# Eight experts with places of their own size, taken in the order of their rows

## The chip, the cores and the metric

The kernel runs on one NeuronCore of a Trainium2 chip. The metric is the device time of one execution in microseconds. Five engines share the work: TensorE (PE, with its weight loads shown as PEld), VectorE (DVE), ScalarE (ACT), GpSimd (POOL) and SyncE (SP), which issues transfers. Each takes its instructions in the order in which they were written into its queue and waits for others by semaphores.

## The reference

Two layers of a post-normalised encoder on 512 tokens of 1024 features, in float32. Each layer mixes tokens (three mixers in parallel, merged by gates) and then channels: the first layer by a dense SwiGLU, the second by eight experts, of which each token takes two. The change is in the experts alone:

```python
def moe_swiglu(h2, w_router, w_gate, w_up, w_down):
    logits = (h2 @ w_router).astype(jnp.float32)
    top_logits, top_idx = lax.top_k(logits, TOP_K)        # TOP_K = 2 of N_EXPERTS = 8
    top_w = jax.nn.softmax(top_logits, axis=-1)
    ...
    hid = jax.nn.silu(lax.ragged_dot(xs, w_gate, sizes)) * lax.ragged_dot(xs, w_up, sizes)
    y = lax.ragged_dot(hid, w_down, sizes)                # D_EXP = 3584
    y = y * top_w.reshape(-1)[order][:, None].astype(y.dtype)
    return jnp.zeros_like(h2).at[tok].add(y.astype(h2.dtype))
```

512 tokens with two experts each make 1024 rows, 128 per expert on average. With the inputs used, the experts 0 to 7 get 136, 132, 144, 108, 129, 114, 124 and 137 rows.

## The kernel before

Mixers, dense FFN and the second mixers take the first 2090 us. The expert stage (function `moe`) takes the rest.

Float32 products are made of two parts. Every weight chunk comes raw by a transfer on SP (`Stream.load`, L191, two chunks of 128x1024 or 128x896 in one, five buffers). ACT rounds it to the product's fp32 format (whi, L204), DVE takes what is left in half precision (wlo, L205). Four chunks of parts exist: the two in use and two ahead. PE multiplies whi with both parts of the rows (2 x 144 columns, `gu<-xg,whi`) and wlo with the rows in half precision (144 columns, `gu<-xh,wlo`), all at L276.

*Routing* (L1139 to L1190): the two best experts of each token as one-hot masks `oh`, their sum `sel`, the place of a token among the rows of its expert `rank`. `gather_rows(e)` makes the row indices of an expert (o1, ii, ix) and reads its rows from DRAM by address (xt, POOL, L1189); `gather_turn` turns them to columns (xg, xh; L1205 to L1208) in two blocks, of 128 and 16 rows.

*Places*: every expert has CAP = 144 rows. If one has more, the loop of L1240 runs `overflow` for 128 further rows of it, as often as the count `nxi` says; with these inputs no round runs.

*An expert* (`expert`, from L1308) has 28 steps f of gate and up: two chunks (gate and up), 32 products into `gu`. After them ACT copies the low part (gt, L1317), DVE adds the high part (gt, L1318), ACT makes the silu (gs, L1320), POOL multiplies by up (gs, L1321), ACT rounds (hd, L1323), DVE takes the rest (hd, L1324) and POOL makes the half-precision copy (hh, L1327). Then 16 pairs of chunks of down: 14 + 14 products a pair into `mx`, with yt (ACT L1345, DVE L1346) after every second pair. `turn_out` turns yt to rows (ys, L1299) and ACT's queue writes them to `ybuf` (L1303), or `ylast` for the last expert (L1301). The next expert's rows are gathered from step 8 on, turned from step 18 on.

*The end*: during the last expert the rows of the other seven are fetched from ybuf (POOL, L1358, eight gathers yg with three buffers) and added with their weights (DVE, acc, L1360). The last expert's own rows follow in two halves (`combine_last`, L1377 to L1383), with the statistics of the norm (L343), and then the last LayerNorm goes to the output.

*What sets the order*: PE's order is the order of the program. The queues of ACT, DVE, POOL and SP are ordered by the compiler's scheduler, which has its own estimates of every instruction's duration. So a change of shapes can change the order in which the engines take their work.

Of the kernel before, what the change touches and what calls it, by code (L numbers as in the profile page):

```python
# [21 lines left out]
P = 128  # L22
# [17 lines left out]
CAP = 144  # L40
# [101 lines left out]
def constants():  # L142
# [23 lines left out]
    c["eidx"] = np.ascontiguousarray(np.broadcast_to(np.stack([NE - e, e * CAP], 0)[None], (P, 2, NE))).astype(np.float32)  # L166
# [7 lines left out]
class Stream:  # L174
    """weight chunks in order of use, each split into a rounded part and the exact rest"""
# [57 lines left out]
def body(tc, A, out, dbg=None):  # L233
# [27 lines left out]
    class PE:  # L261
        """matmuls in the order of emission, with a rough count of the time they take"""
# [25 lines left out]
    def soon(after, fn, *a):  # L288
        """matmul work on results of other engines: run between chunks once they had time to come"""
# [12 lines left out]
            # the task whose results were begun last holds the most buffers  # L302
# [75 lines left out]
    def need(*js):  # L378
        """the token tiles that the next products read"""
# [4 lines left out]
    def settle():  # L384
        """after the first product on a norm's output: its buffers are free"""
# [13 lines left out]
    # feature-major product of one 128-column chunk  # L399
# [10 lines left out]
    # the first chunks after a norm, half of the tokens at a time  # L410
# [18 lines left out]
    # token-major product, n columns, per k-tiles a chunk; the last four chunks a token tile at a time  # L429
# [64 lines left out]
    # ---------------------------------------------------------------- weights  # L494
# [7 lines left out]
    # ------------------------------------------------------------ first norm  # L502
# [53 lines left out]
    def route_consts():  # L556
# [17 lines left out]
        eidx = load_const("eidx", [P, 2, NE], pool=rp_)  # L574
# [82 lines left out]
    def hgrn_head(pool, h, cmask, fkq, v, g):  # L657
        # running products inside blocks that double: c up to t, e after s
# [319 lines left out]
    def overflow(pool, more, pairs, hsrc, acc):  # L978
        """the next P rows of an expert that has more than CAP: which one follows from the count of rounds"""
        step, rounds = more  # L980
# [18 lines left out]
        V.tensor_scalar(at[:, 1:2], at[:, 1:2], float(P), float(CAP), op0=OP.mult, op1=OP.add)  # L999
# [3 lines left out]
        V.tensor_scalar(here, eidx[:, 0], at[:, 0:1], None, op0=OP.is_equal)  # L1003
        ow = pool.tile([P, 3, NJ], F32, name="ow")
# [43 lines left out]
        def load(ap):  # L1048
            raw = pool.tile([P, 2048], F32, name="oraw", bufs=3)
# [45 lines left out]
        y = pool.tile([P, D], F32, name="oy")  # L1095
# [25 lines left out]
    def moe(hT, g_ap, b_ap):  # L1121
# [13 lines left out]
        with tc.tile_pool(name="route", bufs=1, side="right") as mp, ExitStack() as psg_:  # L1135
            hsrc = hbuf[0]
            blocks = [(0, P), (P, CAP - P)]
# [36 lines left out]
            def gather_rows(e):  # L1174
                xts = []
                o1 = mp.tile([P, NJ, CAP], BF, name="o1", bufs=2)
                for j in range(NJ):
                    V.tensor_scalar(o1[:, j], iota, rank[:, j, e:e + 1], sel[:, j, e:e + 1],
                                    op0=OP.is_equal, op1=OP.mult)
                for b0, bn in blocks:  # L1180
# [18 lines left out]
            def gather_turn(xs, xts, b, kk):  # L1199
                (b0, bn), xt, (xg, xh) = blocks[b], xts[b], xs  # L1200
# [10 lines left out]
            turns_in = [(b, kk) for b in range(len(blocks)) for kk in range(2)]  # L1211
            xts = gather_rows(0)
            stream.fill()
            # softmax over the two
# [8 lines left out]
            # rounds of P more rows that the experts need beyond CAP  # L1223
            pc = psM.tile([P, NE], F32, name="mx")
            for j in range(NJ):
                T.matmul(pc, ones, selb[:, j], start=(j == 0), stop=(j == NJ - 1))
            rounds = mp.tile([P, NE], F32, name="rounds")
            V.tensor_scalar(rounds, pc, float(CAP), None, op0=OP.is_gt)
            for r in range(1, (S - CAP + P - 1) // P):
                V.tensor_scalar(ms2, pc, float(CAP + P * r), None, op0=OP.is_gt)  # L1230
                V.tensor_tensor(rounds, rounds, ms2, OP.add)
            nxi = mp.tile([P, 1], I32, name="nxi")
# [6 lines left out]
            n_more = nc.values_load(nxi[0:1, 0:1], min_val=0, max_val=NE * ((S - CAP + P - 1) // P),  # L1239
                                    skip_runtime_bounds_check_because="a sum of comparisons")  # L1240
            with tc.tile_pool(name="over", bufs=1) as op_:
                with tc.For_i(0, n_more, 1):
                    overflow(op_, (step, rounds), (oh, wt, rank, sel), hsrc, acc)

            xg = new_x()
            for b, kk in turns_in:
                gather_turn(xg, xts, b, kk)
            dump("xg", xg[0][:, :, 0].bitcast(F32))
            # rows of the expert outputs, one per choice; the last expert's come separately
# [3 lines left out]
            V.tensor_scalar(ms[:, 4], rank[:, :, NE - 1], float(CAP - 1), None, op0=OP.min)  # L1253
            V.tensor_copy(sl7, ms[:, 4])
            for i in range(2):
                V.tensor_tensor(t1, rank, oh[:, i], OP.mult)
                V.tensor_reduce(ms[:, 4], t1, AX.X, OP.add)
                V.tensor_scalar(ms[:, 5], ms[:, 4], float(CAP), None, op0=OP.is_lt)
# [22 lines left out]
            def flat(ps):  # L1281
                return ps[:, :2 * CAP].rearrange("p (a c) -> p a c", a=2)
# [11 lines left out]
            def turn_out(e, kk, yt, ys):  # L1294
                for (b0, bn), y in zip(blocks, ys):
# [6 lines left out]
                    elif kk:  # L1302
                        SC.dma_start(ybuf[e * CAP + b0:e * CAP + b0 + bn], y[:bn])  # L1303
# [4 lines left out]
            def expert(e, xs, at):  # L1308
                xg, xh = xs
                hid = []  # L1310
                for f in range(KE):
                    ps = psG.tile([P, 2, 512], F32, name="gu", bufs=2)
                    ws = stream.take(2)
                    accumulate([(flat(ps[:, q]), ws[q], lambda k: (xg[:, k], xh[:, k]), True, True)
                                for q in range(2)], KD)
                    t = bp.tile([P, 2, CAP], F32, name="gt", bufs=2)
                    SC.activation(t, ps[:, :, CAP:2 * CAP], AF.Copy)  # L1317
                    V.tensor_tensor(t, ps[:, :, :CAP], t, OP.add)  # L1318
                    s = bp.tile([P, CAP], F32, name="gs", bufs=2)
                    SC.activation(s, t[:, 0], AF.Silu, scale=1.0 / (WS * XS))  # L1320
                    G.tensor_tensor(s, s, t[:, 1], OP.mult)  # L1321
                    hd = bp.tile([P, 2, CAP], FR, name="hd", bufs=KE + 6)
# [3 lines left out]
                    hh = bp.tile([P, CAP], F16, name="hh", bufs=KE + 6)  # L1326
# [5 lines left out]
                for _ in blocks:  # L1332
# [3 lines left out]
                for d in range(KD):  # L1336
                    ps = psM.tile([P, 512], F32, name="mx")
                    pv = flat(ps)
# [119 lines left out]
```

## Time and profile before

| | us |
|---|---|
| three runs | 3321.95, 3325.41 (median), 3325.93 |
| span of the profiled execution | 3321.9 |
| first expert's gate/up begins at | 2124.0 |
| gate/up of an expert, 0 to 7 | 101.3, 96.6, 96.6, 97.5, 96.6, 95.5, 95.5, 105.7 |
| down of an expert | 46.5, the last 53.8 |
| from the last down product to the end | 33.6 |

The profiled execution's span is its own time. The rows that stand in a section below come from this one execution. A view called "timeline" gives start, duration, engine, line, operation, and in brackets the idle time of the engine just before and what ended it. "Windows" gives, for stretches of the span, the busy time of each engine with its number of instructions, the granted clock of TensorE as a share of full speed (1.00 is 2.4 GHz, 0.50 is 1.2 GHz), the busy share of the 16 DMA engines and their GB/s.

### The profile page before, as it was taken

How to read it: one execution, taken by the hardware profiler on the slowest of the kernel's cores; microseconds unless marked ns; L12 is line 12 of the kernel's file. 1: busy time of each engine (PE TensorE's matmuls, PEld its weight loads, DVE VectorE, ACT ScalarE, POOL GpSimd, SP SyncE). 2: the span in 40 equal slices, each digit the busy share in tenths (PEclk: the TensorE clock that was granted, in tenths of full speed). 3: DMA queues.
4: the chain of work that ended last, by engine and by line, in shares of the span. 5: the costliest groups of instructions: out<-in, count | busy, mean ns of one | idle time of the engine just before them, and what ended most of it. 6: DMA issues, size and time to landing. Idle time of an engine off the chain costs nothing. (4 is left out here: it accounts for less than half of the span.)

```text
span 3321.9 us, 53257 instructions
## 1 busy us (share of the span) xinstructions
PE 3167.9 (95%) x20782; PEld 2760.0 (83%) x20782; DVE 2091.5 (63%) x2862; ACT 1737.9 (52%) x2993; POOL 851.4 (26%) x901
## 2 busy tenths in 40 slices
PE   7999899999999999999999999799999999999985
PEld 6778788888888888677788888699999999999985
DVE  5766633344533245667433344698898989889896
ACT  4754323422322225744323322487787878878774
POOL 1233401111100010335201111253342524325253
PEclk9999999999999999999999999799999999999997
DMA  5112232233323332122222223689898898988984
GB/s 175 45 55 88 64 103 70 95 95 126 118 95 99 129 108 95 46 67 70 83 89 83 89 92 117 219 312 329 309 322 320 302 330 311 331 316 313 337 295 179
DMA packets 109588, 566.63 MB, mean 171 GB/s; under 512 B 12624, under 2 KB 12672, under 8 KB 80656
## 3 DMA queue, kind: packets, MB, share of 16 engines
q1 hardware_dynamic: 97344, 522.23, 45.3%
q10 hardware_dynamic: 7344, 25.69, 2.1%
q0 software_dynamic: 4640, 15.22, 1.3%
q8 instruction: 165, 2.70, 0.3%
q14 instruction: 95, 0.78, 0.1%
HBM read 547.89 MB, written 15.20 MB: 170 GB/s over the span
## 5 line engine op out<-in xcount | busy, mean ns | idle before, releaser
L205 DVE SCALAR_TENSOR_TENSOR wlo<-raw,whi 128x1024 f16<-128x1024 f32 (+1 forms) x704 | 858.6, 1246 | 75.6 <-ACT whi L204 75.2
L208 ACT ACTIVATE whi<-raw 128x1024 fp32r<-128x1024 f32 x314 | 332.6, 1060 | 833.5 <-PE acc L276 710.4
L204 ACT ACTIVATE whi<-raw 128x1024 fp32r<-128x1024 f32 (+1 forms) x704 | 707.7, 1012 | 97.3 <-PE mx L276 86.9
L209 DVE TENSOR_TENSOR wlo<-raw,whi 128x1024 fp32r<-128x1024 f32 x314 | 435.5, 1388 | 509.7 <-ACT whi L208 481.2
L276 PE MATMUL gu<-xg,whi 128*128 128x288 f32 x3584 | 536.3, 302 | 24.6 <-DVE gt L1318 23.2
L276 PEld LDWEIGHTS gu<-xg,whi 128*128 128x128 f32 x3584 | 486.6, 189 | 37.2 <-DVE gt L1318 24.2
L276 PE MATMUL acc<-hThi,whi 128*128 128x512 f32 (+1 forms) x1312 | 509.9, 389 | 2.3 <-ACT hThi L326 2.3
L276 PE MATMUL acc<-hTlo,whi 128*128 128x512 f32 (+1 forms) x1312 | 506.4, 386 | 1.6 <-DVE hTlo L327 1.6
L276 PE MATMUL acc<-hThi,wlo 128*128 128x512 f32 (+1 forms) x1312 | 506.2, 386 | 0.0
L1321 POOL TENSOR_TENSOR gs<-gs,gt 128x144 f32<-128x144 f32 x224 | 224.4, 1002 | 576.9 <-ACT gs L1320 546.7
L276 PEld LDWEIGHTS <-wlo 128*128 128x128 f16 x5376 | 333.6, 98 | 39.3 <-DVE wlo L205 13.7
L276 PEld LDWEIGHTS acc<-hThi,whi 128*128 128x128 f32 x1312 | 248.7, 190 | 55.1 <-issue 4.9
L276 PEld LDWEIGHTS acc<-hTlo,whi 128*128 128x128 f32 x1312 | 248.6, 190 | 49.4 <-DVE hTlo L327 1.8
L276 PEld LDWEIGHTS acc<-hThi,wlo 128*128 128x128 f32 x1312 | 248.5, 189 | 49.4
L276 PE MATMUL mx<-hd,whi 128*128 128x288 f32 x1792 | 270.2, 300 | 6.4 <-DVE hd L1324 6.4
L276 PE MATMUL gu<-xh,wlo 128*128 128x144 f16 x3584 | 264.8, 227 | 6.0 <-DVE wlo L205 6.0
L276 PEld LDWEIGHTS mx<-hd,whi 128*128 128x128 f32 x1792 | 241.7, 188 | 8.4 <-DVE hd L1324 8.2
L276 PE MATMUL acc<-whi,hThi 128*128 128x512 f32 (+1 forms) x576 | 224.7, 390 | 0.1
L276 PE MATMUL acc<-whi,hTlo 128*128 128x512 f32 (+1 forms) x576 | 220.5, 383 | 3.3 <-DVE hTlo L327 3.3
L276 PE MATMUL acc<-wlo,hThi 128*128 128x512 f32 (+1 forms) x576 | 220.0, 382 | 2.8 <-DVE wlo L209 2.8
L1327 POOL CAST hh<-hd 128x144 f16<-128x144 f32 x224 | 171.2, 764 | 90.4 <-ACT hd L1323 90.4
L357 POOL TENSOR_TENSOR ln_r<-ln_r,ln_b 128x512 f32<-128x512 f32 x26 | 42.0, 1631 | 446.7 <-DVE ln_r L356 441.5
(263 smaller groups left out, 4554.2 us busy)
## 6 DMA issues: line engine op xcount, KB each, us to landing
raw<-in_w_gu SPq DMA_DIRECT2D x224, 1024.0 KB, 5.3
raw<-in_w_l SPq DMA_DIRECT2D x248, 512.0 KB, 3.5
raw<-in_w_dn SPq DMA_DIRECT2D x128, 896.0 KB, 4.7
raw<-in_w_ffn SPq DMA_DIRECT2D x66, 512.0 KB, 3.5
hspillm<-ln_r ACTq DMA_DIRECT2D x8, 512.0 KB, 2.6
ybuf<-ys ACTq DMA_DIRECT2D x7, 512.0 KB, 4.9
ln_r<-in_x SPq DMA_DIRECT2D x4, 512.0 KB, 10.1
hspillin<-ln_r ACTq DMA_DIRECT2D x4, 512.0 KB, 4.0
```

Of the source, the lines that this page charges most:

```text
L204: nc.scalar.activation(hi[:, :n], raw, AF.Copy, scale=WS)
L205: nc.vector.scalar_tensor_tensor(lo[:, :n], raw, WS, hi[:, :n].bitcast(F32), op0=OP.mult, op1=OP.subtract)
L208: nc.scalar.activation(hi[:, :n], raw, AF.Copy)
L209: nc.vector.tensor_tensor(lo[:, :n], raw, hi[:, :n].bitcast(F32), OP.subtract)
L276: nc.tensor.matmul(out_, lhsT, rhs, start=start, stop=stop)
L357: G.tensor_tensor(r[:, sl], r[:, sl], bb[:, sl], OP.add)
L1321: G.tensor_tensor(s, s, t[:, 1], OP.mult)
L1327: G.tensor_copy(hh, hd[:, 0].bitcast(F32))
```

## The change

The eight experts get places of 144, 144, 140, 136, 132, 126, 118 and 112 rows. Expert 0 comes first as before. The seven others are sorted on the chip by their counts of rows (key, place, perm, order): the one with most rows takes the second place, and so on. SP reads each place's expert number from `order` into a register and loads its weights from the address that follows. The masks and ranks are permuted to places (`by_place`). An expert with more rows than its place has gives rounds of `overflow` as before, now against its own size. Buffers of hd and hh go from 34 to 32, oraw from 3 to 2. Lines that carry only comments are left out of the diff.

```diff
-CAP = 144
+CAPS = (144, 144, 140, 136, 132, 126, 118, 112)
+CAP = max(CAPS)
+ROW0 = [sum(CAPS[:i]) for i in range(len(CAPS))]
...
-        for e in range(NE):
-            stream.add([A["w_gu"][e, f] for f in range(KE)], 2)
-            stream.add([A["w_dn"][e, d, c] for d in range(KD) for c in range(2)], 2)
+        def add_expert(e):
+            def of(w):
+                return w.rearrange("o p c -> (o p) c")
+            stream.add([of(A["w_gu"][e, f]) for f in range(KE)], 2)
+            stream.add([of(A["w_dn"][e, d, c]) for d in range(KD) for c in range(2)], 2)
+        add_expert(slice(0, 1))
...
+            key = mp.tile([P, NE], F32, name="key")
+            V.scalar_tensor_tensor(key, pc, float(NE), eidx[:, 0], op0=OP.mult, op1=OP.add)
+            G.memset(key[:, 0:1], 2.0 * NE * (S + 1))
+            cmp = mp.tile([P, NE, NE], F32, name="cmp")
+            V.tensor_tensor(cmp, key[:, None, :].broadcast_to([P, NE, NE]),
+                            key[:, :, None].broadcast_to([P, NE, NE]), OP.is_gt)
+            place = mp.tile([P, NE], F32, name="place")
+            V.tensor_reduce(place, cmp, AX.X, OP.add)
+            perm = mp.tile([P, NE, NE], F32, name="perm")
+            V.tensor_tensor(perm, place[:, None, :].broadcast_to([P, NE, NE]),
+                            eidx[:, 1, :, None].broadcast_to([P, NE, NE]), OP.is_equal)
...
+            V.tensor_tensor(cmp, perm, eidx[:, 1:2].broadcast_to([P, NE, NE]), OP.mult)
+            V.tensor_reduce(key, cmp, AX.X, OP.add)
+            order = mp.tile([P, NE], I32, name="order")
+            V.tensor_copy(order, key)
...
+            prod = mp.tile([P, NJ, NE, NE], F32, name="prod")
+            def by_place(t):
+                V.tensor_tensor(prod, t[:, :, None, :].broadcast_to([P, NJ, NE, NE]),
+                                perm[:, None].broadcast_to([P, NJ, NE, NE]), OP.mult)
+                V.tensor_reduce(t, prod, AX.X, OP.add)
...
+            for e in range(1, NE):
+                add_expert(bass.ds(nc.values_load(order[0:1, e:e + 1], engines=[mybir.EngineType.SP], min_val=0, max_val=NE - 1,
+                                                  skip_runtime_bounds_check_because="a place in an order"), 1))
+            for t in (oh[:, 0], oh[:, 1], sel, rank):
+                by_place(t)
...
             def expert(e, xs, at):
                 xg, xh = xs
+                cap = CAPS[e]
...
-                    accumulate([(flat(ps[:, q]), ws[q], lambda k: (xg[:, k], xh[:, k]), True, True)
+                    accumulate([(flat(ps[:, q], cap), ws[q], lambda k: (xg[:, k, :, :cap], xh[:, k, :cap]), True, True)
                                 for q in range(2)], KD)
-                    t = bp.tile([P, 2, CAP], F32, name="gt", bufs=2)
-                    SC.activation(t, ps[:, :, CAP:2 * CAP], AF.Copy)
-                    V.tensor_tensor(t, ps[:, :, :CAP], t, OP.add)
-                    s = bp.tile([P, CAP], F32, name="gs", bufs=2)
+                    t = bp.tile([P, 2, CAP], F32, name="gt", bufs=2)[:, :, :cap]
+                    SC.activation(t, ps[:, :, cap:2 * cap], AF.Copy)
+                    V.tensor_tensor(t, ps[:, :, :cap], t, OP.add)
+                    s = bp.tile([P, CAP], F32, name="gs", bufs=2)[:, :cap]
```

The same cut to `cap` rows is made in hd, hh, yt and in the blocks of gather and turn-out (one block in place of two where `cap` is at most 128).

The scheduler gives other orders to the changed kernel. Line numbers move by some 50 (L204 is L208, L205 is L209, L1317 is L1372, L1318 is L1373, L1320 is L1375, L1323 is L1378, L1324 is L1379, L1327 is L1382).

ACT in step 10 of the seventh expert (index 6, 118 rows now), before; the numbers behind names tell buffers of different steps apart:

```order
L1323 ACTIVATE hd_31631<-gs_31628 128x144
L1317 ACTIVATE gt_31679<-gu_31636 128x288
L204 ACTIVATE whi_31747<-raw_31745 128x1024
L1320 ACTIVATE gs_31682<-gt_31679 128x144
L204 ACTIVATE whi_31751<-raw_31745 128x1024
L1323 ACTIVATE hd_31685<-gs_31682 128x144
L1317 ACTIVATE gt_31733<-gu_31690 128x288
```

and the same place now:

```order
L208 ACTIVATE whi_31669<-raw_31667 128x1024
L208 ACTIVATE whi_31673<-raw_31667 128x1024
L1372 ACTIVATE gt_31655<-gu_31612 128x2x118
L1375 ACTIVATE gs_31658<-gt_31655 128x118
L1378 ACTIVATE hd_31661<-gs_31658 128x118
L208 ACTIVATE whi_31723<-raw_31721 128x1024
L208 ACTIVATE whi_31727<-raw_31721 128x1024
```

Both whi of a step now come first, and gt, gs and hd of one step follow each other without another instruction between. Experts 5, 6 and 7 have this order in nearly all steps; experts 0 to 4 keep the one of before.

DVE at the same place, before:

```order
L1318 TENSOR_TENSOR gt_31679<-gu_31636,gt_31679 128x288
L205 SCALAR_TENSOR_TENSOR wlo_31698<-raw_31691,whi_31697 128x1024
L205 SCALAR_TENSOR_TENSOR wlo_31748<-raw_31745,whi_31747 128x1024
L1324 SCALAR_TENSOR_TENSOR hd_31685<-gs_31682,hd_31685 128x144
L1318 TENSOR_TENSOR gt_31733<-gu_31690,gt_31733 128x288
```

and now:

```order
L209 SCALAR_TENSOR_TENSOR wlo_31670<-raw_31667,whi_31669 128x1024
L1373 TENSOR_TENSOR gt_31655<-gu_31612,gt_31655 128x2x118
L209 SCALAR_TENSOR_TENSOR wlo_31674<-raw_31667,whi_31673 128x1024
L1379 SCALAR_TENSOR_TENSOR hd_31661<-gs_31658,hd_31661 128x118
L209 SCALAR_TENSOR_TENSOR wlo_31724<-raw_31721,whi_31723 128x1024
```

gt has moved between the two wlo of a step; hd of the same step follows behind the second wlo.

POOL at the start of the last expert, before (yg are the gathers from ybuf, L1358, now L1413; gs is the product with up, hh the copy):

```order
L1321 TENSOR_TENSOR gs_33402<-gs_33402,gt_33399 128x144
L1358 DMA yg_33788<-ybuf_17643,sl_17614 128x1024
L1327 CAST hh_33408<-hd_33405 128x144
L1358 DMA yg_33899<-ybuf_17643,sl_17614 128x1024
L1358 DMA yg_34010<-ybuf_17643,sl_17614 128x1024
L1321 TENSOR_TENSOR gs_33456<-gs_33456,gt_33453 128x144
L1327 CAST hh_33462<-hd_33459 128x144
L1321 TENSOR_TENSOR gs_33510<-gs_33510,gt_33507 128x144
```

and now:

```order
L1382 CAST hh_33293<-hd_33290 128x112
L1413 DMA yg_33734<-ybuf_17698,sl_17665 128x1024
L1413 DMA yg_33845<-ybuf_17698,sl_17665 128x1024
L1413 DMA yg_33956<-ybuf_17698,sl_17665 128x1024
L1376 TENSOR_TENSOR gs_33348<-gs_33348,gt_33345 128x112
L1382 CAST hh_33354<-hd_33351 128x112
L1413 DMA yg_34067<-ybuf_17698,sl_17665 128x1024
L1413 DMA yg_34178<-ybuf_17698,sl_17665 128x1024
L1413 DMA yg_34289<-ybuf_17698,sl_17665 128x1024
L1376 TENSOR_TENSOR gs_33402<-gs_33402,gt_33399 128x112
```

Before, five of the eight gathers were spread over the later steps, one in every second; now three come before the product of step 1, three before that of step 2 and two before that of step 3.

DVE near the end of the last expert's down product, before (wlo are weight parts for PE, BN_STATS the statistics of the last norm; these are listed without buffer numbers, x3 is three in a row):

```order
L205 SCALAR_TENSOR_TENSOR wlo<-raw,whi 128x896 x3
L343 BN_STATS ln_st<-acc 128x6 x2
L205 SCALAR_TENSOR_TENSOR wlo<-raw,whi 128x896
L1346 SCALAR_TENSOR_TENSOR yt<-mx,yt 128x144
L205 SCALAR_TENSOR_TENSOR wlo<-raw,whi 128x896
L343 BN_STATS ln_st<-acc 128x6 x2
L1346 SCALAR_TENSOR_TENSOR yt<-mx,yt 128x144
```

and now:

```order
L209 SCALAR_TENSOR_TENSOR wlo<-raw,whi 128x896 x3
L347 BN_STATS ln_st<-acc 128x6 x4
L209 SCALAR_TENSOR_TENSOR wlo<-raw,whi 128x896
L1401 SCALAR_TENSOR_TENSOR yt<-mx,yt 128x112
L209 SCALAR_TENSOR_TENSOR wlo<-raw,whi 128x896 x4
L1401 SCALAR_TENSOR_TENSOR yt<-mx,yt 128x112
L209 SCALAR_TENSOR_TENSOR wlo<-raw,whi 128x896
```

Two wlo stood behind the first two BN_STATS; now six stand behind all four.

## Rows read from the trace of the kernel before

**Rows 1.** The page: span, busy time by engine

```profile
span 3321.9 us, 53257 instructions
...
PE 3167.9 (95%) x20782; PEld 2760.0 (83%) x20782; DVE 2091.5 (63%) x2862; ACT 1737.9 (52%) x2993; POOL 851.4 (26%) x901
```

**Rows 2.** Windows: from:to, length, busy by engine, clock, DMA share, GB/s

```profile
2092.16:2124.01 31.85, 15.74 (x89) 14.09 (x88) 20.44 (x82) 10.47 (x16) 7.14 (x9) 0.50 0.61 229
...
2844.86:2940.36 95.50, 93.92 (x933) 90.37 (x930) 89.97 (x118) 79.22 (x143) 49.95 (x58) 1.00 0.88 311
2940.36:2986.82 46.46, 45.68 (x460) 44.22 (x458) 37.68 (x44) 34.46 (x47) 3.10 (x4) 1.00 0.94 339
...
3128.76:3234.49 105.73, 93.87 (x909) 88.59 (x906) 93.56 (x116) 77.36 (x138) 52.82 (x60) 1.00 0.85 313
```

**Rows 3.** Timeline, a steady gate/up step: start, us, engine, line, operation

```profile
2466.45 0.32 ACT L1320 ACTIVATE gs<-gt 128x144 f32<-128x144 f32 x1 [0.21 <-DVE gt L1318]
...
2469.23 0.44 DVE L1318 TENSOR_TENSOR gt<-gu,gt 128x288 f32<-128x288 f32 x1
2469.60 1.21 DVE L205 SCALAR_TENSOR_TENSOR wlo<-raw,whi 128x1024 f16<-128x1024 f32 x1
2469.71 0.32 ACT L1320 ACTIVATE gs<-gt 128x144 f32<-128x144 f32 x1 [0.21 <-DVE gt L1318]
```

**Rows 4.** Timeline between the routing and the first expert

```profile
2105.93 0.19 DVE L1157 TENSOR_TENSOR t<-lg,ms 128x32 f32<-128x32 f32 x1
...
2108.18 0.19 DVE L1164 TENSOR_TENSOR selb<-oh 128x32 bf16<-128x32 f32 x1
...
2113.03 0.14 DVE L1234 CAST nxi<-nx 128x1 int32<-128x1 f32 x1
```

**Rows 5.** Timeline, one chunk pair of a down product

```profile
2529.17 2.09 PE L276 MATMUL mx<-hd,whi 128*128 128x288 f32 x14
...
2531.11 1.05 PE L276 MATMUL mx<-hh,wlo 128*128 128x144 f16 x14
```

**Rows 6.** Timeline of PE, fp32 products of 256 columns

```profile
150.05 0.28 PE L276 MATMUL mx<-skl,sqt 128*128 128x256 f32 x1
150.17 0.28 PE L276 MATMUL mx<-skh,sqt 128*128 128x256 f32 x1
```

**Rows 7.** Windows, the burst of weight loads ahead of the experts

```profile
2090.00:2100.00 10.00, 9.04 (x47) 8.48 (x47) 7.69 (x13) 4.05 (x7) 0.00 (x0) 0.61 0.97 392
```

**Rows 8.** Timeline of expert 7, where ACT takes both whi in a row

```profile
3206.38 2.35 DVE L205 SCALAR_TENSOR_TENSOR wlo<-raw,whi 128x1024 f16<-128x1024 f32 x2
...
3207.36 0.39 ACT L1317 ACTIVATE gt<-gu 128x288 f32<-128x288 f32 x1
3207.60 1.48 POOL L1321 TENSOR_TENSOR gs<-gs,gt 128x144 f32<-128x144 f32 x1 [2.81 <-ACT gs L1320]
...
3209.11 0.32 ACT L1323 ACTIVATE hd<-gs 128x144 fp32r<-128x144 f32 x1 [1.36 <-POOL gs L1321]
3209.34 1.99 ACT L204 ACTIVATE whi<-raw 128x1024 fp32r<-128x1024 f32 x2
3209.47 0.31 DVE L1324 SCALAR_TENSOR_TENSOR hd<-gs,hd 128x144 fp32r<-128x144 f32 x1 [0.74 <-ACT hd L1323]
```

**Rows 9.** Timeline of POOL, start of expert 7

```profile
3141.41 1.54 POOL L1358 DMA_INDIRECT yg<-ybuf,sl  x1 [2.24 <-DMA ybuf<-ys]
...
3145.76 0.51 POOL L1321 TENSOR_TENSOR gs<-gs,gt 128x144 f32<-128x144 f32 x1
```

**Rows 10.** Tile yg in expert 7: its gathers from issue to landing

```profile
DMA to landing us min/median/max: 5.3/7.0/8.9
```

**Rows 11.** Timeline of the last expert's down product, near its end

```profile
3279.45 0.69 DVE L343 BATCH_NORM_STATS2 ln_st<-acc 128x6 f32<-128x512 f32 x1 [4.39 <-POOL acc L1381]
...
3283.83 1.25 POOL L1381 TENSOR_TENSOR acc<-acc,xt 128x512 f32<-128x512 f32 x1
...
3286.09 1.02 PE L276 MATMUL mx<-hh,wlo 128*128 128x144 f16 x7 [5.32 <-DVE wlo L205]
```

More of the change, by code (lines that the diff above doesn't have):

```diff
@@ L978, in overflow @@
     def overflow(pool, more, pairs, hsrc, acc):
-        step, rounds = more
+        step, rounds, capE = more
         oh, wt, rank, sel = pairs
@@ L1003, in overflow @@
         V.tensor_scalar(here, eidx[:, 0], at[:, 0:1], None, op0=OP.is_equal)
+        V.tensor_tensor(past, here, capE, OP.mult)
+        V.tensor_reduce(at[:, 0:1], past, AX.X, OP.add)
+        V.scalar_tensor_tensor(at[:, 1:2], at[:, 1:2], float(P), at[:, 0:1], op0=OP.mult, op1=OP.add)
         ow = pool.tile([P, 3, NJ], F32, name="ow")
@@ L1136, in moe, with blocks_of @@
             hsrc = hbuf[0]
-            blocks = [(0, P), (P, CAP - P)]
+            def blocks_of(e):
+                return [(b0, min(P, CAPS[e] - b0)) for b0 in range(0, CAPS[e], P)]
             lg = mp.tile([P, NJ, NE], F32, name="lg")
@@ L1177, in gather_rows @@
                 for j in range(NJ):
-                    V.tensor_scalar(o1[:, j], iota, rank[:, j, e:e + 1], sel[:, j, e:e + 1],
+                    V.tensor_scalar(o1[:, j, :CAPS[e]], iota[:, :CAPS[e]], rank[:, j, e:e + 1], sel[:, j, e:e + 1],
                                     op0=OP.is_equal, op1=OP.mult)
-                for b0, bn in blocks:
+                for b0, bn in blocks_of(e):
                     pi = psM.tile([P, 2], F32, name="mx")
@@ L1197, in new_x, with gather_turn @@
                 return xg, xh
-            def gather_turn(xs, xts, b, kk):
-                (b0, bn), xt, (xg, xh) = blocks[b], xts[b], xs
+            def gather_turn(e, xs, xts, b, kk):
+                (b0, bn), xt, (xg, xh) = blocks_of(e)[b], xts[b], xs
                 tp = psM.tile([P, 4, P], F32, name="mx")
@@ L1209, in gather_turn, with turns_in @@
                               xg[:, 4 * kk:4 * kk + 4, 0, b0:b0 + bn].bitcast(F32))
-            turns_in = [(b, kk) for b in range(len(blocks)) for kk in range(2)]
+            def turns_in(e):
+                return [(b, kk) for b in range(len(blocks_of(e))) for kk in range(2)]
             xts = gather_rows(0)
@@ L1238, in moe @@
             G.memset(acc, 0.0)
-            n_more = nc.values_load(nxi[0:1, 0:1], min_val=0, max_val=NE * ((S - CAP + P - 1) // P),
+            n_more = nc.values_load(nxi[0:1, 0:1], min_val=0, max_val=NE * MORE,
                                     skip_runtime_bounds_check_because="a sum of comparisons")
@@ L1242, in moe @@
                 with tc.For_i(0, n_more, 1):
-                    overflow(op_, (step, rounds), (oh, wt, rank, sel), hsrc, acc)
-            xg = new_x()
-            for b, kk in turns_in:
-                gather_turn(xg, xts, b, kk)
+                    overflow(op_, (step, rounds, capE), (oh, wt, rank, sel), hsrc, acc)
+            prod = mp.tile([P, NJ, NE, NE], F32, name="prod")
[3 more added lines that the diff above has]
+                V.tensor_reduce(t, prod, AX.X, OP.add)
+            xg = new_x()
+            for b, kk in turns_in(0):
+                gather_turn(0, xg, xts, b, kk)
+            for e in range(1, NE):
[3 more added lines that the diff above has]
+                by_place(t)
             dump("xg", xg[0][:, :, 0].bitcast(F32))
@@ L1294, in turn_out @@
             def turn_out(e, kk, yt, ys):
-                for (b0, bn), y in zip(blocks, ys):
+                for (b0, bn), y in zip(blocks_of(e), ys):
                     tp = psM.tile([P, 4, P], F32, name="mx")
@@ L1331, in expert @@
                 ys = []
-                for _ in blocks:
+                for _ in blocks_of(e):
                     y = bp.tile([P, D], F32, name="ys", bufs=2)
@@ L1391, in moe @@
                     at[GATHER] = [lambda: rows_.extend(gather_rows(e + 1))]
-                    for n, (b, kk) in enumerate(turns_in):
-                        at[GATHER + 10 + 2 * n] = [lambda b=b, kk=kk: gather_turn(nxt, rows_, b, kk)]
+                    for n, (b, kk) in enumerate(turns_in(e + 1)):
+                        at[GATHER + 10 + 2 * n] = [lambda b=b, kk=kk: gather_turn(e + 1, nxt, rows_, b, kk)]
                 else:
```

51 lines of the change are left out of this document (29 added, 22 removed).

## The prediction, made before the changed kernel ran

> **What bounds the kernel now.** I read the page's busy times first. TensorE (PE) is busy 95% of the span and the vector engine DVE only 63% [rows 1], so at first sight fewer rows per expert should pay. The table of windows, one window for each phase of an expert, says otherwise: in the 95.50 us of expert 5's gate/up phase DVE is busy 89.97 us and PE 93.92, at clock 1.00; in its down phase DVE is busy 37.68 of 46.46 and PE 45.68 [rows 2]. So gate/up has two engines near their limit and only down is PE's alone. The timeline of one gate/up step shows a period of 3.26 us (silu to silu, 2466.45 to 2469.71) [rows 3]. ACT's queue there alternates: a silu or a rounding stands between two weight roundings (whi), so a product that POOL hands back late holds up nothing.
>
> The orders of instructions were the last thing read, and the forecast rests on them. Experts 0 to 4 (144 to 132 rows) keep that alternation. Experts 5 to 7 (126, 118, 112) do not: ACT has both whi, then gt, gs and hd of one and the same step. An in-order engine then waits for DVE and for POOL inside each step.
>
> **The change, part by part.** All sums start from the profiled span of 3321.9 us, which lies by the lowest of the three runs (3321.95) and 3.5 us under their median.
>
> *Start: +6 us (3 to 12).* Ahead of the loop count nxi stand 20 DVE rows in place of nine. Ten dependent small ones took 2105.93 to 2108.18, 0.225 us each [rows 4]: 11 x 0.225 = 2.5. Behind the loop 13 products and sums by place (256 elements and their sums) come before or between the first gathered columns; bound by 0.23 and by the 0.44 of a 288-element row [rows 3] they are 3.0 to 5.7, part of it beside the four transposed blocks. I take 3.5. The seven loads of an expert's number stand on SP, which waits for buffers most of the time; nothing else is queued there but the weight loads, which are up to five ahead. At worst a load delays one weight transfer by about a microsecond seven times, hence the 12.
>
> *Gate/up of experts 2 to 4: -3 us (-10 to 0).* PE gets shorter, but DVE's two wlo of 1.21 us do not depend on the rows; only gt and hd shrink.
>
> *Down of experts 2 to 6: -19 us (-27 to 0).* A chunk pair goes from 2529.17 to about 2531.96: 1.94 us for 14 fp32 products, 0.85 for 14 half-precision ones [rows 5], 0.139 and 0.061 each. Products of 256 columns start 0.120 us apart [rows 6], so 128 rows in place of 144 save 14 x 0.019 + 14 x 0.007 = 0.36 us a pair, 5.8 per expert of 16 pairs; 126 rows about 5.3 to 6, and experts 2, 3, 4 with 4, 8, 12 rows fewer 1.2, 2.4, 3.5. DVE's 37.68 us per phase [rows 2] are the floor, about 2.36 a pair, so expert 6 saves 6.5 and no more than 7: 1.2 + 2.4 + 3.5 + 5.3 + 6.5 = 19. Transfers could be the floor instead: the phase has its DMA engines 0.94 busy at 339 GB/s, while a burst ahead of the experts ran at 392 over 10 us [rows 2, 7]. From the rows I take no DMA floor above DVE's.
>
> The Trainium skill (HBM Reference, Specifications (TRN2)) gives about 358 GB/s as a core's share and some 425 for a core that streams alone. Held to 358, a pair of 0.92 MB could not go below 2.56 us, an estimate from that page, and experts 5 and 6 would save 3.7 each: the sum would be 4 us higher. The burst's 392 speaks for the second figure.
>
> *Gate/up of experts 5 to 7: +74 us.* One period by hand, in ACT's new order, from whi to whi. Two whi take 1.99 and the next instruction starts some 0.09 before their end: 1.90 [rows 8]. gt 0.39 at 288 columns, 0.37 at 252: 2.27. DVE starts 0.04 after an ACT result (3209.43 to 3209.47) [rows 8], 2.31. DVE's next instruction starts 0.37 after gt (2469.23 to 2469.60) [rows 3], 0.33 for the smaller one: 2.64. That next one is the second wlo, 1.21: 3.86. Meanwhile ACT's silu is done at about 3.1 and POOL's product could start, but the trace shows the product ending only after DVE's wlo: wlo ended at 3208.73, the product, 1.48 us long, at 3209.08 [rows 8], 0.35 later. So 4.19 here. ACT's hd starts 0.03 later and the next whi 0.23 after that [rows 8]: 4.45. With 118 and 112 rows 4.41 and 4.38. PE needs under 3 us of it, so the chain decides. 28 steps make 124.6, 123.5 and 122.6 us against 95.5, 95.5 and 105.73 [rows 2]: +29.1, +28.0, +16.9. (Expert 6's phase was as long as expert 5's.) The ends lie at 3.26 (no loss) and, where the product is not held, at 3.9; see the rivals.
>
> The Trainium skill (SBUF — State Buffer, Who interferes with whom) says DVE and POOL share a port pair by an exclusive lock, so that the loser is blocked for the whole instruction, and that the order of issue decides. The row of 1.48 us agrees: 0.51 is what a product took with DVE out of the way. Where the wlo comes first, the rule gives the 4.45; if the product ever came first, it would be 3.9 and DVE would pay. In the new order the wlo is first by some 0.4 us.
>
> *From gate/up to down: +6 us (0 to 12).* hd of the last step is now late for the second chunk pair; about 2 us in each of three experts.
>
> *Last expert's gathers: +19 us (10 to 35).* POOL now has the eight gathers in three clumps between the products of steps 0 to 3, and DVE has the sums in clumps of 3, 3 and 2. The first waits for the write of expert 6's rows (2.24 us now [rows 9]); each takes 5.3 to 8.9 us to land, median 7.0 [rows 10], and there are three buffers. Landing (7.0) plus the sum (about a wlo, 1.2) less the rest of a period gives 4 to 6 us a clump: three of 5, and 4 for the first wait. Taken with the least and the greatest landing and buffers in series: 10 to 35.
>
> *End: +1 us (-3 to +5).* Expert 7's first ten down pairs save 4. Then four BN_STATS stand in one piece on DVE ahead of six wlo. Now the first pair waited 4.39 us for POOL and PE 5.32 for the wlo behind it; POOL's last sum starts at 3283.83, 4.4 us after the first [rows 11]. Six weight parts wait for that one now: +7 (4 to 10). One block less to turn and write: -2.
>
> Sum: 6 - 3 - 19 + 74 + 6 + 19 + 1 = +84; 3321.9 + 84 = 3406 us.
>
> **The rivals.** *Product not held (R2).* If POOL's product runs beside the wlo at 0.51 [rows 9], the period is 2.31 + 0.42 (gt) + 0.04 + 0.32 (silu) + 0.03 + 0.51 + 0.26 = 3.9. 84 steps x 0.51 = 43 less: 3363. Against it stands the 1.48 row; for it, that timings drift and DVE's wlo may itself be late for its weights.
>
> *Low clock (R3).* PE would be busy some 60% of three phases. Between routing and experts, 15.74 busy of 31.85, the granted clock was 0.50, that is 1.2 of 2.4 GHz [rows 2]. At half clock a step of 118 rows needs twice its 2.6 us, 5.2, so it would then be PE-bound, 0.8 above the chain. Half of 84 steps: +34, and some microseconds in each down phase: 3450. Against it: expert 7 had steps with PE waiting and kept 1.00 over its phase [rows 2].
>
> *The rows pay (R1, other side).* The chain only matters if its period exceeds 3.26. Were ACT's late work covered (the product finished before the second wlo starts, gt and silu beside the whi), gate/up would go by DVE, 2 x 1.21 + 0.33 + 0.35, about 3.1: -14 over 84 steps, -7 for expert 7's slow steps, and with +6 - 3 - 19 + 2 the end is 3287. For it: ACT has only 79 of 95 us of work. Against: the order as written makes gs wait for gt and hd for gs with nothing between.
>
> *An overflow round (R4).* If an expert had more rows than its place, the row loop would run. The router's counts on these inputs, sorted behind the first (136), are 144, 137, 132, 129, 124, 114, 108, all within 144, 140, 136, 132, 126, 118, 112. A round re-reads a whole expert, 28 + 16 loads at 3.26 and 2.79 us at least, 136: over 3450.
>
> **How the numbers follow.** Forecast 0.65, R2 0.12, R3 0.12, R1 0.09, R4 0.02. The forecast's own terms give 3380 to 3440 (start, downs, gathers and end at their ends, not all at once). The range takes R2 in mostly and the lower part of R3: 3355 to 3448. A change under 0.2%, 6.6 us, can't be told from none. Faster is R1 (0.09), no change lies between R1 and R2 and has 0.02, slower 0.89.
>
> **What would show it.** In the changed profile, windows of experts 5 to 7's gate/up should be 120 to 126 us long with DVE at about 70% and PE about 65%, ACT's hd waiting for POOL's gs in nearly each of 84 steps, and the POOL product ending 0.35 after DVE's second wlo. Experts 0 to 4 should stay at 3.2 us a step; their down windows shrink by 1 to 4 us. The last expert should show steps of 10 us and more beside the gathers. A window under 95 us in experts 5 to 7 refutes the chain; 109 us would be R2; a clock under 0.9 there R3.

## The result, and the profile after

The changed kernel takes 3399.12 us (median of four runs, 3397.44 to 3401.97) against 3324.57 before: a ratio of 1.0228, 95% interval 1.0213 to 1.0242. It is slower, as forecast; the profiled execution has a span of 3395.6 us, 73.7 more than before, where the prediction's sum gave 84.

The page of the changed kernel, to be set against [rows 1]: TensorE does 60 us less and idles 134 us more (span less busy time: 288 against 154).

```profile
span 3395.6 us, 53797 instructions
...
PE 3107.5 (92%) x20722; PEld 2697.5 (79%) x20722; DVE 2070.1 (61%) x2874; ACT 1718.3 (51%) x2981; POOL 810.7 (24%) x893
```

Windows of the changed kernel, columns as in [rows 2]: gate/up of expert 4, gate/up and down of expert 5, gate/up of expert 6, gate/up and down of expert 7.

```profile
2699.23:2791.64 92.41, 87.69 (x920) 83.16 (x918) 88.14 (x118) 77.25 (x140) 48.32 (x55) 1.00 0.90 325
2835.06:2954.24 119.18, 86.86 (x921) 81.40 (x918) 83.59 (x112) 76.31 (x138) 39.46 (x55) 1.00 0.73 254
2954.24:2997.86 43.62, 40.97 (x457) 39.70 (x454) 37.92 (x45) 33.96 (x49) 2.45 (x4) 1.00 0.91 346
2997.86:3114.96 117.10, 83.67 (x917) 78.55 (x914) 82.43 (x112) 74.87 (x137) 37.94 (x55) 0.99 0.73 257
3156.72:3301.89 145.17, 83.03 (x905) 78.28 (x902) 89.78 (x117) 73.43 (x135) 42.99 (x60) 0.89 0.67 236
3301.89:3363.33 61.44, 43.82 (x458) 42.45 (x456) 38.37 (x47) 30.79 (x45) 15.10 (x16) 0.81 0.56 200
```

Expert 4, with 132 rows and the old order of ACT, is 4.2 us shorter than before; expert 5, with 126 rows and the new one, is 27 us longer than expert 4 although no engine has more to do. A gate/up step of expert 5 on ACT, DVE, POOL and PE shows why, the counterpart of [rows 3] and [rows 8]:

```profile
2903.02 0.31 ACT L1378 ACTIVATE hd<-gs 128x126 fp32r<-128x126 f32 x1 [1.14 <-POOL gs L1376]
2903.24 1.99 ACT L208 ACTIVATE whi<-raw 128x1024 fp32r<-128x1024 f32 x2
...
2905.13 0.36 ACT L1372 ACTIVATE gt<-gu 128x252 f32<-128x252 f32 x1
2905.52 0.42 DVE L1373 TENSOR_TENSOR gt<-gu,gt 128x252 f32<-128x252 f32 x1
2905.86 1.22 DVE L209 SCALAR_TENSOR_TENSOR wlo<-raw,whi 128x1024 f16<-128x1024 f32 x1
2905.98 0.31 ACT L1375 ACTIVATE gs<-gt 128x126 f32<-128x126 f32 x1 [0.49 <-DVE gt L1373]
...
2906.00 2.16 PE L280 MATMUL gu<-xg,whi 128*128 128x252 f32 x16 [1.34 <-DVE gt L1373]
2906.43 0.95 POOL L1376 TENSOR_TENSOR gs<-gs,gt 128x126 f32<-128x126 f32 x1 [2.63 <-ACT gs L1375]
2907.42 0.31 ACT L1378 ACTIVATE hd<-gs 128x126 fp32r<-128x126 f32 x1 [1.13 <-POOL gs L1376]
2907.64 1.99 ACT L208 ACTIVATE whi<-raw 128x1024 fp32r<-128x1024 f32 x2
```

From whi to whi it is 4.40 us, and in it ACT waits 0.49 for DVE and 1.13 for POOL. POOL's product ends at 2907.38, 0.30 after DVE's wlo (2907.08). PE waits 1.34 for DVE's gt. Over experts 5 and 6 ACT waits 65.5 us for POOL, 56 times, once in every step:

```profile
ACT hd L1378 <- POOL gs L1376: 65.5, 56, 1.8
ACT gs L1375 <- DVE gt L1373: 24.3, 51, 0.5
```

Expert 7's gathers on POOL's timeline, the counterpart of [rows 9]; from the view of the chain that ended last, the write of expert 6's rows, from its issue to its landing; and two windows, the second of the stretch in which that write ends:

```profile
3180.96 1.00 POOL L1413 DMA_INDIRECT yg<-ybuf,sl  x1 [17.89 <-DMA ybuf<-ys]
...
3187.02 0.99 POOL L1413 DMA_INDIRECT yg<-ybuf,sl  x1 [1.35 <-DVE acc L1415]
3190.09 1.73 POOL L1413 DMA_INDIRECT yg<-ybuf,sl  x1 [2.08 <-DVE acc L1415]
```

```profile
3160.66 19.45 DMA ybuf<-ys
```

```profile
3160.60:3172.00 11.40, 7.47 (x91) 7.08 (x89) 4.40 (x6) 3.06 (x7) 1.30 (x2) 1.00 0.94 379
3172.00:3181.00 9.00, 0.00 (x0) 0.00 (x0) 0.00 (x0) 0.00 (x0) 0.04 (x1) 0.52 0.11 45
```

For nine microseconds every engine stands still while 11% of the DMA engines' time, about two of 16, moves 45 GB/s. The granted clock is 0.52 there. And the end of the last down product, the counterpart of [rows 11]:

```profile
3347.91 0.69 DVE L347 BATCH_NORM_STATS2 ln_st<-acc 128x6 f32<-128x512 f32 x1 [11.39 <-POOL acc L1436]
...
3352.27 1.25 POOL L1436 TENSOR_TENSOR acc<-acc,xt 128x512 f32<-128x512 f32 x1
...
3355.30 0.84 PE L280 MATMUL mx<-hh,wlo 128*128 128x112 f16 x7 [14.44 <-DVE wlo L209]
```

### The profile page after: what moved, and what is told of

It is laid out like the page before. It is cut to its first block, busy times and chain, and to the rows that moved or that the text cites. A ratio compares the mean times of both kernels' runs of the same rounds, so it can differ in the third digit from the quotient of the medians.

```text
span 3395.6 us, 53797 instructions
## 1 busy us (share of the span) xinstructions
PE 3107.5 (92%) x20722; PEld 2697.5 (79%) x20722; DVE 2070.1 (61%) x2874; ACT 1718.3 (51%) x2981; POOL 810.7 (24%) x893
## 5 line engine op out<-in xcount | busy, mean ns | idle before, releaser
L209 DVE SCALAR_TENSOR_TENSOR wlo<-raw,whi 128x1024 f16<-128x1024 f32 (+1 forms) x704 | 838.3, 1212 | 104.3 <-ACT whi L208 96.5
L208 ACT ACTIVATE whi<-raw 128x1024 fp32r<-128x1024 f32 (+1 forms) x704 | 693.4, 1010 | 90.5 <-PE mx L280 67.8
L280 PE MATMUL gu<-xg,whi 128*128 128x288 f32 (+6 forms) x3584 | 506.2, 294 | 145.7 <-DVE gt L1373 139.4
L280 PEld LDWEIGHTS gu<-xg,whi 128*128 128x128 f32 x3584 | 459.9, 191 | 168.8 <-DVE gt L1373 159.5
L1376 POOL TENSOR_TENSOR gs<-gs,gt 128x144 f32<-128x144 f32 (+6 forms) x224 | 216.6, 967 | 655.2 <-ACT gs L1375 640.4
L280 PEld LDWEIGHTS <-wlo 128*128 128x128 f16 x5376 | 310.6, 98 | 36.4 <-DVE wlo L209 17.6
L280 PE MATMUL mx<-hd,whi 128*128 128x288 f32 (+6 forms) x1792 | 256.9, 294 | 12.5 <-DVE hd L1379 9.7
L280 PE MATMUL gu<-xh,wlo 128*128 128x144 f16 (+6 forms) x3584 | 245.7, 222 | 1.1 <-DVE wlo L209 1.0
L280 PEld LDWEIGHTS mx<-hd,whi 128*128 128x128 f32 x1792 | 230.9, 192 | 14.8 <-DVE hd L1379 11.4
L1382 POOL CAST hh<-hd 128x144 f16<-128x144 f32 (+6 forms) x224 | 144.6, 646 | 90.6 <-ACT hd L1378 90.5
L1378 ACT ACTIVATE hd<-gs 128x144 fp32r<-128x144 f32 (+6 forms) x224 | 70.2, 313 | 164.1 <-POOL gs L1376 163.2
```

The lines of the kernel that those rows point to most:

```text
L208: nc.scalar.activation(hi[:, :n], raw, AF.Copy, scale=WS)
L209: nc.vector.scalar_tensor_tensor(lo[:, :n], raw, WS, hi[:, :n].bitcast(F32), op0=OP.mult, op1=OP.subtract)
L280: nc.tensor.matmul(out_, lhsT, rhs, start=start, stop=stop)
L1378: SC.activation(hd[:, 0], s, AF.Copy, scale=1.0 / WS)
L1382: G.tensor_copy(hh, hd[:, 0].bitcast(F32))
```

## The experiments

Each ran beside the kernel before, whose median was 3323.9 to 3324.7 us in these groups. The first gate/up product begins between 2124.0 and 2133.5 us in the eleven profiled executions, and part of that spread lies ahead of every edit; so the phases are compared, and a span of one run only with that in mind.

**The sorting alone.** Diff: `CAPS = (144,) * 8` in the changed kernel.

> All eight places keep 144 rows; the sorting, the masks by place and the weights by address stay. ACT keeps its alternating order in experts 0 to 6. If sorting costs only its start, the first gate/up product comes 5 to 6 us later than before and the phases are as before: 3321.9 + 6 = 3328 for the span, ratio 1.001 to 1.003. If loads by address slow the weight stream, each expert's phases are longer and the span passes 3340.

Measured: 3327.25 us, ratio 1.0012 (1.0002 to 1.0022), span 3321.9 in the profiled run. Expert 5's gate/up is what it was, to the hundredth in length:

```profile
2845.10:2940.59 95.49, 93.92 (x932) 90.36 (x930) 89.95 (x118) 79.25 (x143) 50.27 (x58) 1.00 0.88 311
```

The first product begins at 2126.75, 2.7 us later than before and not 5 to 6: from the first row of the routing [rows 4] to it the time grew by 4.8, while what lies ahead was 2.1 shorter in this execution. Sorting and loads by address cost under 0.25% together; the loss is in the sizes and the orders that came with them.

**More rows for the last three.** Diff: `CAPS = (144, 144, 140, 136, 132, 132, 132, 132)`.

> Places of 144, 144, 140, 136 and four times 132: experts 5 to 7 get more rows than in the changed kernel (126, 118, 112), and ACT's order alternates again in most of their steps. If the chain in ACT's order is what costs, gate/up of experts 5 and 6 takes 92 to 96 us as in expert 4 (92.4), not 119 and 117, expert 7 about 100, and the span is about 3295 (3285 to 3310), some 100 below the changed kernel. If smaller tiles, or one block in place of two, cost in themselves, it stays within 30 us of 3396. If PE's columns decided, it would be slower than the changed kernel.

Measured: 3311.05 us, ratio 0.9958 (0.9944 to 0.9972), span 3309.2. Experts 5 and 6:

```profile
2837.45:2931.80 94.35, 88.17 (x932) 83.89 (x930) 88.59 (x118) 77.45 (x143) 48.51 (x59) 1.00 0.90 329
2974.86:3068.05 93.19, 88.11 (x933) 83.85 (x930) 86.21 (x117) 77.09 (x143) 48.76 (x58) 1.00 0.89 320
```

Adding 6, 14 and 20 rows made the kernel 88 us faster. Expert 7 took 106.6 us, not 100, so the span is at the upper end of what was expected. ACT has the alternating order (hd, gt, whi, gs, whi) in 10 and 13 of the 28 steps of experts 5 and 6 and variants of it in most others; in expert 7 mostly hd, whi, whi, gs, gt, where gs and hd of a step have the next gt between them. This changes rows and order together; the next two change the order alone.

**hd behind the next two whi.** Diff in the changed kernel, for experts 5 to 7 (an order on ACT without any wait; `queue(a, b)` puts a behind b; the main lines, with comments that explain them):

```diff
+                    turn = e >= 5 and f >= 2
+                    if turn:
+                        stream.behind = steps[f - 2][:2]        # each whi of this take behind gt, gs of step f - 2
                     ws = stream.take(2)
+                    if turn:
+                        stream.behind = []
+                        queue(steps[f - 2][2], stream.last)      # and hd of step f - 2 behind the second whi
...
```

> The changed kernel, with the same rows and instructions; only ACT's order in gate/up of experts 5 to 7 is set by hand so that hd of a step stands behind the next two whi. A period by hand: two whi 1.90, hd 0.22, gt 0.34, handing to DVE and back with DVE's gt 0.48, gs 0.22: 3.16 us. The chain theory expects gate/up of experts 5 and 6 at 88 to 92 us against 119 and 117, expert 7 about 115 (its gathers stay in clumps), the span about 3310. If it is POOL's held product that costs and not the waiting behind it, the period stays above 4 us and the span above 3370.

Measured: 3310.98 us, ratio 0.9955 (0.9939 to 0.9972), span 3312.6. Gate/up of experts 5, 6 and 7:

```profile
2837.92:2930.52 92.60, 86.02 (x921) 81.17 (x918) 83.13 (x113) 74.68 (x139) 40.44 (x55) 1.00 0.91 325
2973.03:3059.70 86.67, 81.47 (x917) 77.21 (x914) 82.22 (x113) 72.93 (x138) 39.84 (x55) 1.00 0.95 352
3101.94:3220.24 118.30, 83.36 (x904) 78.69 (x902) 89.53 (x118) 71.63 (x136) 43.52 (x60) 0.87 0.79 289
```

Same rows, same instructions: 27, 30 and 27 us less, expert 6 below the 88 to 92 expected, expert 5 just above. The order was the cause. The scheduler moved DVE's queue along: gt, wlo, wlo, hd as before the change, where the changed kernel has gt, wlo, hd, wlo. What ACT's order and what DVE's costs alone was not separated.

**The old alternation.** As above, with gs also behind the first whi, so that ACT has gt, whi, gs, whi, hd.

> The changed kernel with ACT's order in gate/up of experts 5 to 7 set by hand to the one before the change: gt, whi, gs, whi, hd. The chain theory expects what DVE needs, two wlo and the two small ones, 3.0 to 3.1 us a step: 86 to 90 us for experts 5 and 6, the span about 3305, and the gathers of expert 7 the largest loss left. If the order were only a symptom and shorter matmuls starve PE otherwise, the phases stay above 110 us.

Measured: 3314.11 us, ratio 0.9964 (0.9952 to 0.9977).

```profile
2837.44:2931.24 93.80, 86.67 (x920) 82.48 (x918) 86.46 (x113) 76.70 (x139) 48.14 (x55) 0.98 0.91 321
2975.27:3063.49 88.22, 82.64 (x917) 78.68 (x914) 85.32 (x113) 75.60 (x138) 47.44 (x55) 0.98 0.95 344
```

Expert 6 came as expected, expert 5 took 93.8 and not 86 to 90, and the profiled span is 3315.4 and not 3305. Two different orders on ACT bring the steps back; what they share is that hd no longer stands directly behind its product, and DVE's gt, wlo, wlo, hd.

**The write of expert rows, cut.** Diff: the write of bn rows to ybuf is issued as two, of `bn // 16 * 16` rows and the rest.

> The changed kernel with each write of an expert's rows to ybuf cut at a multiple of 16 rows (126 as 112 and 14, 118 as 112 and 6). In the changed kernel the write of 118 rows was issued at 3160.66 and POOL's gathers went at 3180.96, while the last ten of these microseconds had the DMA engines 0.1 busy at about 50 GB/s. If the 118 rows are spread over one or two DMA engines only, the cut write lands within 6 to 9 us, POOL's wait of 17.9 us falls to 4 to 6, and the span to about 3383. If the write was late because weight loads stood ahead of it, the wait stays at 15 us or more and the span within 4 us of 3396.

Measured: one run, 3383.11 us, span 3381.3. The larger part lands 8.4 us after its issue, and POOL's first gather waits 6.9, a little above the 4 to 6 expected:

```profile
3169.21 1.01 POOL L1416 DMA_INDIRECT yg<-ybuf,sl  x1 [6.89 <-issue]
```

The view of DMA from 3155 to 3185 us has the queue of this write (packets, MB, share of 16 engines), in the changed kernel and then in this run:

```profile
q10 hardware_dynamic: 120, 0.48, 3.9%
...
q10 hardware_dynamic: 140, 0.48, 4.0%
```

In both runs 118 of the packets are the rows of 4 KB. In the changed kernel the trace has them from 3164.16 to 3179.77, never more than three at a time; in this run from 3163.32 to 3167.54, up to 13 at a time. Expert 7's gate/up went from 145.17 to 133.4, 11.0 of it in this wait. How the rows were cut, not the weight loads ahead, made the write slow. (The scheduler also moved the third gather behind the product of step 1.) Of the span's 14.3 us, 3.9 lie ahead of the first product.

**The second wlo in halves.** Diff: in gate/up of experts 5 to 7 DVE makes each second wlo by two instructions of 512 columns.

> The changed kernel with the second wlo of each gate/up step of experts 5 to 7 made by two DVE instructions of half the width, ACT's order as it is. If POOL's product is held by the DVE instruction that runs, it gets its turn after the first half (0.6 us earlier): product about 0.5 to 0.6 us long, period 3.8 in place of 4.4 us, 84 x 0.55 = 46 us less, span 3350. If the product takes 0.95 us for another reason, the period stays at 4.4 to 4.5 and the span at 3396 or above.

Measured: one run, 3360.54 us, span 3358.6, nine above what was expected. The timeline of a step of expert 5 and of the end of the step before:

```profile
2899.65 0.46 POOL L1382 TENSOR_TENSOR gs<-gs,gt 128x126 f32<-128x126 f32 x1 [2.75 <-ACT gs L1381]
2899.68 0.97 DVE L213 SCALAR_TENSOR_TENSOR wlo<-raw,whi 128x512 f16<-128x512 f32 x1
...
2900.35 1.99 ACT L209 ACTIVATE whi<-raw 128x1024 fp32r<-128x1024 f32 x2
...
2902.98 1.58 DVE L213 SCALAR_TENSOR_TENSOR wlo<-raw,whi 128x512 f16<-128x512 f32 x2
2903.09 0.31 ACT L1381 ACTIVATE gs<-gt 128x126 f32<-128x126 f32 x1 [0.49 <-DVE gt L1379]
2903.55 0.46 POOL L1382 TENSOR_TENSOR gs<-gs,gt 128x126 f32<-128x126 f32 x1 [2.75 <-ACT gs L1381]
2904.04 0.31 ACT L1384 ACTIVATE hd<-gs 128x126 fp32r<-128x126 f32 x1 [0.64 <-POOL gs L1382]
2904.26 1.99 ACT L209 ACTIVATE whi<-raw 128x1024 fp32r<-128x1024 f32 x2
```

The product takes 0.46 in place of 0.95, the two halves 1.58 in place of 1.22, and the period is 3.90 (2900.35 to 2904.26 from whi to whi). That is the price that the prediction gave for a product that isn't held. The Trainium skill (SBUF — State Buffer, Who interferes with whom) says the two engines share ports by a lock that is kept for a whole instruction, and that the one that issues first keeps the other out. The traces agree: in the changed kernel the wlo starts first (2905.86, the product 2906.43) and the product takes 0.95; here the product starts first (2899.65, the second half 2899.68), takes 0.46, and the half takes 0.97 where the first half of a step takes 0.68.

**BN_STATS last.** Diff: the four BN_STATS of the first halves stand behind DVE's last yt.

> The changed kernel with the four early BN_STATS of the last norm set behind DVE's last yt, so that no wlo stands behind POOL's sums. If that queue is what stretched the last down phase, it goes from 61.4 to 39 to 42 us and the rest after it grows by at most 3: span 3376 to 3380. If the low clock there (0.81) came first, the phase stays above 50.

Measured: one run, 3378.96 us, span 3377.2. The last down phase and what follows it:

```profile
3298.52:3341.46 42.94, 40.09 (x458) 39.17 (x456) 35.93 (x43) 30.81 (x45) 7.78 (x10) 0.96 0.77 283
3341.46:3377.20 35.74, 0.66 (x5) 0.22 (x2) 21.91 (x34) 7.55 (x13) 21.04 (x17) 0.58 0.27 97
```

The phase is 18.5 us shorter (42.94, 0.9 above the range), what follows 3.5 longer; the clock in the phase is 0.96 and not 0.81, so the low clock came of the wait. The span is 18.4 less, and 5.3 of that lie ahead of the first product.

**All orders together**, with the write cut, and the memset that the sort waits for on DVE.

> All four together on the changed kernel's sizes: hd behind the next two whi in experts 5 to 7, the write cut, the eight gathers of the last expert one in every second step from step 4 on with each sum three steps later, BN_STATS behind the last yt, and the memset ahead of the sort on DVE in place of POOL (2.4 us of waiting there). Terms on the run with hd later (3312.6): gathers and write -21, end -18, memset -2: 3272 (3262 to 3285), faster than before by 1.1 to 1.8 per cent. If the gathers only move their wait to DVE's sums (8 x 1.28 us more on DVE, which limits the steps), expert 7's gate/up stays above 105 us and the span above 3280.

Measured: 3273.41 us, ratio 0.9846 (0.9830 to 0.9863), span 3277.4. Gate/up of experts 5, 6, 7 and the last down:

```profile
2835.95:2928.69 92.74, 87.07 (x921) 82.68 (x918) 83.17 (x113) 74.62 (x139) 40.20 (x55) 0.98 0.92 320
2972.73:3060.43 87.70, 82.01 (x916) 77.36 (x914) 82.21 (x113) 73.05 (x138) 39.38 (x55) 1.00 0.94 346
3101.06:3198.94 97.88, 83.39 (x905) 79.30 (x902) 89.80 (x117) 72.48 (x137) 43.19 (x60) 0.95 0.93 351
3198.94:3240.65 41.71, 39.81 (x458) 39.04 (x456) 34.59 (x42) 29.64 (x43) 7.46 (x9) 0.96 0.78 286
```

It beats both kernels: 126 us under the changed one, 50 (1.5%) under the one before.

**Equal places with the same orders.** Diff: `CAPS` as eight times 144 in the kernel above.

> The kernel with all orders set, but eight equal places of 144 rows: what the sizes themselves are worth once the order is not in their way. From the phases of the two traces (experts 2 to 6: 14 us of down and 19 of gate/up; expert 7: about 6 of gate/up and 7 of down) the sizes should be worth 46 us: span about 3320 (3312 to 3326), no clear change against before. If the orders alone made the gain, it comes out within 10 us of 3275.

Measured: 3313.03 us, ratio 0.9964 (0.9951 to 0.9976), span 3314.2; six below the expected middle, inside the range. So the orders are worth some 12 us at 144 rows with the sorting paid, and the sizes 40 us (3313.0 to 3273.4) once the order lets them. One reservation: the edit holds hd back but lets a whi stand between gt and gs, and at 144 rows the scheduler put it there in most steps of experts 5 to 7, as in the run with the old alternation. On the smaller places these two orders differ by 1.2 to 2.1 us a phase (92.60 and 93.80, 86.67 and 88.22, 118.30 and 120.36 for experts 5, 6 and 7), little beside the 40.

## Why the prediction was right

| term | predicted | measured, span against span |
|---|---|---|
| start to the first product | +6 | +6.9, of which 1.3 lie ahead of the expert stage |
| gate/up of experts 0, 1 | 0 | -1.9 |
| gate/up of experts 2 to 4 | -3 | -9.1 (-1.1, -3.8, -4.2) |
| down of experts 2 to 6, with the hand-over (+4) | -15 | -13.2 |
| gate/up of experts 5 and 6 | +57 | +45.3 |
| gate/up of expert 7 with its gathers | +36 | +39.4 |
| down of expert 7, hand-over, end | +3 | +6.3 |
| sum | +84 | +73.7 |

*The sum* is nearer than its terms: 17.9 us too much in experts 0 to 6, 7.6 too little in the start, expert 7 and the end.

*The start* was right by luck. From the first row of the routing to the count nxi the time grew by 3.9 us and not 2.5, because DVE waits 2.42 for a memset on POOL that had no term; behind the count it grew by 1.9 and not 3.5. The rest lies ahead of the routing.

*The chain.* The period by hand was 4.45, 4.41 and 4.38 us; the trace has 4.40, 4.35 and 4.31. Each link came as worked out: DVE's next instruction 0.34 after gt, wlo 1.22, the product 0.30 behind it (0.35 was taken), hd 0.04 later, whi 0.22 after hd. That the order and not the sizes costs is shown by the run with hd later, and that the held product is half a microsecond of it by the run with halves. What was mis-sized is the number of periods: 28 were counted, but expert 5 has only 24 in the chain. Its second and third step and its last took 2.86 to 2.87 us, since their weights were ready before or nothing follows: 119.2 and not 124.6 us. So both windows end just under the 120 to 126 us named as the sign.

*The fewer rows.* In experts 2 to 4 the claim that DVE bounds the step, so that rows bring next to nothing, failed: 4.2 us came back in expert 4. The rows did it: sorted but with 144 rows, experts 2 to 4 took 96.6 to 96.7 us. PE was nearer its limit than DVE (93.92 and 89.97 of 95.50 us busy, [rows 2]); that shorter products pay for this reason is argued and not tested. In down 13.2 us came back; without the 3.4 for which PE waited for hd in experts 5 and 6 (4 were taken) it is about 16.5, where 19 was worked out.

*Expert 7.* The gathers were priced at 19 (10 to 35). With 28 periods of 4.31 less the short ones at the ends (about 6), the phase would have been 115, so they cost 30. That the phase came within 4 us of its sum is luck: the chain took 8 less, the gathers 11 more. The three clumps were seen in the order of POOL; that the first would wait 17.9 us for a write of 118 rows was not (4 was taken), and cutting the write gave 11.8 back.

*The end.* +7 for the BN_STATS was the right mechanism, a little small: PE waited 14.44 us in place of 5.32. In both kernels the wait ends 1 to 2 us after POOL's last sum, and that sum ends 20.5 us after the write of the first half is issued (3333.00 to 3353.52; before, 19.9, 3265.22 to 3285.08). But PE now stops 7.9 us after that write and not 15.6, since the BN_STATS stand four weight parts earlier in DVE's queue and the down pairs are shorter. Before, it was the first weight part behind the BN_STATS that kept PE waiting: it ran 4.73 us, where such a part takes 1.08, while POOL made its sums.

```profile
3281.30 4.73 DVE L205 SCALAR_TENSOR_TENSOR wlo<-raw,whi 128x896 f16<-128x896 f32 x1
```

Setting the BN_STATS behind yt gave 15 us in all.

*The rivals.* The product that isn't held (R2) was excluded by the trace and then brought about by the run with halves: 3358.6 against the 3363 given for it. The low clock (R3) did not come over the chain: 1.00 and 0.99 in experts 5 and 6 at 73% and 71% busy PE (some 60% was taken). It came in the standstill of expert 7 (0.52 there, 0.89 over the phase). That the rows pay (R1) needed another order. With hd later alone the span was 3312.6; with the gathers, the write, the BN_STATS and the memset moved too, 3277.4. The 3287 worked out for R1 had no cost for gathers and end, so only the second is its case. No extra round ran (R4): the products into gu are 3584 with each part of the rows, as before.

On the rate of weights: the Trainium skill (HBM Reference, Specifications (TRN2)) gives 358 GB/s as a core's share with both cores streaming. The stretch from 3160.6 moved 379 over 11.4 us here, so for this single core that figure was no ceiling.

## What to carry to other kernels

When shapes change under a scheduler that orders by its own estimates, read the new order of every engine before counting what the smaller shapes save; a step's last link put in front of the next step's first can turn a hidden latency into the period. An instruction that waits for another engine costs little as long as enough useful work stands between it and its producer in the same queue: here ACT's hd waited 1.13 us in a step with nothing between, 0.18 with one whi, not at all with two. And where one engine's queue mixes the feed of TensorE with work that waits for a slow chain, the second belongs behind the first.

## What was not expected of the hardware

- A DRAM write of 118 rows of 4 KB landed 19.5 us after its issue at 3160.66, the last eight of them with 0.11 of the DMA engines busy at 45 GB/s; cut into 112 and 6 rows, the larger part landed in 8.4 us. The packets show the one at most three at a time, the other at up to 13. Writes of 128 rows landed in 4.2 to 6.1 us before.
- A memset of one column on POOL held the sort up by 2.4 us: DVE's compare at 2114.80 waited for it, and it stood behind two gathers whose issue takes POOL 1.04 and 0.87 us. On DVE, in the run with all orders, it took 0.06, and the stretch from the routing's first row to the count was 2.1 us shorter:

```profile
2114.80 0.23 DVE L1249 TENSOR_TENSOR cmp<-key 128x64 f32<-128x64 f32 x1 [2.42 <-POOL key L1247]
```

- POOL's sums and DVE's weight parts hold each other up in both directions: a product took 0.95 us behind a running wlo and 0.46 ahead of it, and a wlo that began while the sums of the end ran took 4.73 us and not 1.08.
